# Start-up loads of a two-layer encoder: issued later, and in another order

## The chip, the core and the metric

The kernel runs on one core of one Trainium2 chip. The metric is the device time of one execution in microseconds (us); less is better. The kernel before was timed three times: 567.24, 567.74 and 567.70 us, median 567.7 us. One more execution was profiled; it took 567.6 us, of which the profile's span (first to last instruction) is 565.8 us. All times "at" which something happens below are us from the start of that span.

The engines are named as the profile names them: PE is the matrix engine (PEld its weight loads), DVE the vector engine, ACT the scalar engine, POOL GpSimd, and SP the engine that here does nothing but issue DMAs. "SPq", "POOLq" and "ACTq" are DMAs issued by these engines. In the DMA parts q1 is SP's queue, q10 is ACT's and q0 is POOL's.

## What is computed

A trunk of two residual layers on one sequence of 256 tokens of width 1024, all in float32:

```python
for layer in range(2):
    hn = rms_norm(h, norm_mix_g[layer])
    if layer == 0:
        proj = hn @ ab_w_in                       # q, k, v of mixers A and B
        o_a = gqa_attention(rope(rms(qa)), rope(rms(ka)), va)
        o_b = dilated_attention(qb, kb, vb, rel_bias)
        mix = concat([o_a, o_b]) @ ab_w_out
    else:
        mix = mla_attention(hn, ...) @ c_w_out
    h = h + mix
    hn = rms_norm(h, norm_mlp_g[layer])
    h = h + square(relu(hn @ mlp_w1[layer])) @ mlp_w2[layer]
return rms_norm(h, final_norm_g)
```

The first product of layer 0 needs the input x twice: transposed and multiplied by the norm's gain (that feeds PE), and as token rows (their sums of squares give the norm's factor 1/rms, which is applied behind the product).

## The kernel before

All weights are packed on the host into 1-MiB chunks of 128 partitions x 2048 numbers, in the order of their use: chunks 0 and 1 are the query weights of mixer A ("qA"), chunk 2 its key and value weights ("kvA"), chunks 3 to 6 the query and key weights of mixer B ("qkB"), and so on. The change's title counts them from one: its third and fourth chunk are chunks 2 and 3 here.

A chunk goes through three steps. SP loads it into one of three buffers (tile `raw`, RAW_BUFS = 3). ACT casts a piece of 512 or 1024 columns to the matrix engine's format (`whi`, line 224, `cast_piece`). DVE subtracts that from the raw piece (`wlo`, line 231, `low_piece`). PE then forms each product from three matmuls, hi x hi, hi x lo and lo x hi (`mm3`, lines 277 to 279). When the last piece of chunk i has been split, `low_piece` issues the load of chunk i + 3 into the buffer that has come free (lines 232 and 233).

Each engine works through its instructions in the order in which the program writes them, and so does each DMA issuer. In layer 0 that order is written by hand (`tc.manual_schedule()`): first a loop over kk = 0 to 7 (lines 983 to 1001), one step per 128 rows of x; in each step ACT casts one piece of chunk 0 or 1 and one row block of x, DVE makes the low parts of both, and PE does 6 matmuls of 512 columns. Then kvA with chunk 2, in four quarters `kv(0)` to `kv(3)`, with chunk 3's pieces cast in between, and then a long string of letters (`ORDER_AB`), each a small step.

What is loaded in the first 20 us, beside the chunks:

- `xgt`, x transposed with the gains, in five parts (ACT's queue and SP's);
- `kc`, 0.5 MiB of constants: rotary tables, and the identity matrix for PE's transposes. POOL multiplies its tables with the gains `gaq` (`tables`, lines 782 to 789) into `tab` (tile `early`), which DVE's rotary step `rope_a` (lines 751 to 761) reads;
- `xh`, the token rows of x, 1 MiB. ACT squares them (`squares`, line 345, four instructions: two behind the second piece of chunk 3, two behind the third);
- POOL's three: `gaq` (64 KB), `oh` (66 KB) and `rb` (1 KB), lines 739 to 741. The last two feed one small matmul at line 1022.

Two waits are added by hand. `hold(dma, ins)` (line 298) makes a DMA's issue wait until the instruction `ins` has ended; before the change it is used once, for chunk 2 behind the cast of step kk = 2 (line 991). SP issues in order, so what stands behind a held DMA waits with it.

Of the kernel before, what the change touches and what calls it, by code (L numbers as in the profile page):

```python
# [20 lines left out]
P = 128  # L21
# [13 lines left out]
NUM_BUCKETS = 32  # L35
# [135 lines left out]
def encoder(ctx: ExitStack, tc: tile.TileContext, x, xg, wall, grow, const, onehot, relb, out):  # L171
    nc = tc.nc
    cp = ctx.enter_context(tc.tile_pool(name="cp", bufs=1))
    wp = ctx.enter_context(tc.tile_pool(name="wp", bufs=1))
    ap = ctx.enter_context(tc.tile_pool(name="ap", bufs=1))
# [10 lines left out]
    def s_bank():  # L186
        return psum("s", 2)
# [4 lines left out]
    def o_bank():  # L192
        return psum("o", 2)
# [9 lines left out]


    raws, parts, done = {}, {}, set()
    at = {"take": 0, "piece": 0, "quarter": 0, "low": [], "hand": True}

    def load(i, pieces=1):
        if i >= N_CH:
            return  # L210
        raws[i] = wp.tile([P, CW], F32, name="raw", tag="raw", bufs=RAW_BUFS)
        for q in range(pieces):
            s = slice(q * CW // pieces, (q + 1) * CW // pieces)
            nc.sync.dma_start(raws[i][:, s], wall[i, :, s])

    def cast_piece(cast=nc.scalar.copy):

# [8 lines left out]
    def low_piece():  # L226

        i, q, n = at["low"].pop(0)
        hi, lo = parts[i, q // 2]
        s = slice(512 * (q % 2), 512 * (q % 2 + n))  # L230
        nc.vector.tensor_tensor(lo[:, s], raws[i][:, 512 * q:512 * (q + n)], hi[:, s].bitcast(F32), op=OP.subtract)  # L231
        if q + n == 4:
            load(i + RAW_BUFS)

    def split_piece(cast=nc.scalar.copy):
        cast = cast_piece(cast)
        low_piece()
        return cast
# [16 lines left out]
    def take(name, j, n, whole=True):  # L255

        i = at["take"]
        assert ORDER[i] == (name, j), (ORDER[i], name, j)
        at["take"] += 1
        while whole and at["piece"] < 4 * i + 4:  # L260
            split_piece()

        def operand(k, c=slice(None)):
            half, kk = divmod(k, n // 2)
            return tuple(z.rearrange("p (k c) -> p k c", k=n // 2)[:, kk, c] for z in parts[i, half])

        return i, operand
# [6 lines left out]
    def mm3(out, a, b, first, last):  # L274

        (ah, al), (bh, bl) = a, b
        nc.tensor.matmul(out, ah, bh, start=first, stop=False)  # L277
        nc.tensor.matmul(out, ah, bl, start=False, stop=False)  # L278
        return nc.tensor.matmul(out, al, bh, start=False, stop=last)  # L279
# [4 lines left out]
    def tok(z, k, t):  # L284
        return pair(z, ALL, k, cols(t))
# [5 lines left out]
    def xT(k):  # L291
        return xgt[:, N_G + k * S:N_G + k * S + S]
# [5 lines left out]
    def hold(dma, ins):  # L298

        tc.add_manual_dep(dma.ins, ins.ins.name, mybir.DependencyInfo(  # L300
            mybir.DependencyClass.Sync, mybir.DependencyReason.DATA), reason="hold")
# [9 lines left out]
    kc = cp.tile([P, N_K], F32, name="kc")  # L311
    xh = cp.tile([P, NT, D], F32, name="xh")
# [231 lines left out]
    later = Later()  # L544
# [169 lines left out]
    with tc.tile_pool(name="l0", bufs=1) as lp:  # L714
# [10 lines left out]
        gaq = early[:, 4 * P:]  # L725
# [4 lines left out]
        rb = lp.tile([NUM_BUCKETS + 1, HB], F32, name="rb")  # L730
        OT = [ap.tile([P, KT, S], F32R, name=f"OT{i}", tag=f"OT{i}") for i in range(2)]

        oh = sp.tile([P, 512], F32, name="oh", tag="prob", bufs=3)
        nc.vector.memset(rb, 1.0)
        for s in range(2):
            other = slice(64 - 64 * s, 128 - 64 * s)
            nc.gpsimd.memset(klA[other, s].bitcast(F32), 0.0)
            nc.gpsimd.memset(klB[other, s::2].bitcast(F32), 0.0)
        nc.gpsimd.dma_start(gaq, bass.AP(tensor=grow.tensor, offset=grow.offset, ap=[[0, P], [1, P]]))
        nc.gpsimd.dma_start(oh[:NUM_BUCKETS + 1, :], onehot)  # L740
        nc.gpsimd.dma_start(rb[:NUM_BUCKETS, :], relb)

        bias = {}

# [37 lines left out]
        def tables():  # L782
            for gi in range(2):
                for t in range(NT):
                    cs, sn = kc[:, K_COSA + 64 * t:K_COSA + 64 * t + 64], kc[:, K_SINA + 64 * t:K_SINA + 64 * t + 64]
                    gv = gaq[:, cols(gi, 64)]
                    nc.gpsimd.tensor_tensor(tab[:, 2 * gi, t], cs, gv, op=OP.mult)
                    nc.gpsimd.tensor_tensor(tab[:, 2 * gi + 1, t, 0:32], sn[:, 0:32], gv[:, 32:64], op=OP.mult)
                    nc.gpsimd.tensor_tensor(tab[:, 2 * gi + 1, t, 32:64], sn[:, 32:64], gv[:, 0:32], op=OP.mult)

        def sums_q(t):
            sq = work()
            nc.scalar.activation(sq, acc[t], AF.Square)
            nc.vector.reduce_sum(sums[:, t, 2:10], sq.rearrange("p (h e) -> p h e", e=64), axis=AX.X)
# [34 lines left out]
        def rope_q(t):  # L829
            qr[t] = sp.tile([P, 512], F32, name="qr", tag="prob", bufs=3)  # L830
            rope_a(qr[t], acc[t], HA, 0, t)
# [146 lines left out]
        with tc.manual_schedule():  # L978
            spin = s_bank()
            for _ in range(N_SPIN):  # L980
                nc.tensor.matmul(spin, idle[:, :P], idle, start=True, stop=True)
            nc.gpsimd.tensor_copy(g, xgt[:, :N_G])
            for j in range(2):
                i, w = take("qA", j, 4, whole=False)
                for k in range(4):
                    kk = 4 * j + k
                    gc = xgt[:, G_MIX + kk:G_MIX + kk + 1]
                    cast = split_piece(nc.scalar.copy if kk else nc.vector.tensor_copy)
                    if kk == 2:
                        raws[2] = wp.tile([P, CW], F32, name="raw", tag="raw", bufs=RAW_BUFS)  # L990
                        hold(nc.sync.dma_start(raws[2], wall[2]), cast)
                        nc.sync.dma_start(kc, const)
                    if kk == 4:
                        nc.sync.dma_start(xh, x.rearrange("(t p) d -> p t d", p=P))
                    nc.scalar.activation(hT[0][:, kk], xT(kk), AF.Copy, scale=gc)  # L995
                    nc.vector.scalar_tensor_tensor(hT[1][:, kk], xT(kk), gc, hT[0][:, kk].bitcast(F32),
                                                   op0=OP.mult, op1=OP.subtract)
                    for t in range(NT):
                        mm3(acc[t], tok(hT, kk, t), w(k), kk == 0, kk == 7)
                    at["quarter"] += 1  # L1000
                done.add(i)
            tables()
            i, w = take("kvA", 0, 8, whole=False)

            def kv(q):
                for k in (2 * q, 2 * q + 1):
                    for t in range(NT):
                        mm3(acckv[t][:, :S], tok(hT, k, t), w(k), k == 0, k == 7)
                if q == 3:
                    done.add(i)  # L1010
                at["quarter"] += 1

            def split(n):
                for _ in range(n):
                    split_piece()

            split(4)
            for t in range(NT):
                sums_q(t)
            kv(0)  # L1020
            lines = o_bank()
            nc.tensor.matmul(lines[:HB, :], rb, oh[:NUM_BUCKETS + 1, :], start=True, stop=True)
            split(1)
            rope_q(0)
            kv(1)
            line_d = dp.tile([HB, 2 * S], F32, name="line_d")
            ls = sp.tile([P, 512], F32, name="ls", tag="pts", bufs=3)
            nc.scalar.copy(ls[:HB, :], lines[:HB, :])
            nc.gpsimd.dma_start(line_d, ls[:HB, :])
            split(1)  # L1030
            squares(part, 0, 0)
            squares(part, 0, 1)
            kv(2)
            split(1)
            squares(part, 1, 0)
            squares(part, 1, 1)
            kv(3)
            rope_q(1)
            sums_k()
            norms()  # L1040
            oacc = {}
            steps = {"a": b0, "b": qk_b(1), "v": v_b(), "o": out_first("outA", OT, oacc),
                     **attention_steps([head_a(h) for h in range(HA)] + [head_b(h) for h in range(HB)], OT)}
            once = {"c": cast_piece, "l": low_piece, "d": spread_d, "s": spread, "n": norms_end, "m": scales,
                    "q": lambda: turn_q(0), "r": lambda: turn_q(1), "k": turn_k, "u": values_a, "x": scale_k,
                    "p": lambda: [rope_a(kr[:, t], acckv[t][:, :P], 2, 2, t) for t in range(NT)],
                    "i": lambda: [load_bias(j) for j in range(2)]}
            for c in "".join(ORDER_AB).replace(" ", ""):
                next(steps[c]) if c in steps else once[c]()
            assert all(next(z, "end") == "end" for z in steps.values()) and not at["low"]  # L1050
# [6 lines left out]
    with tc.tile_pool(name="l1", bufs=1) as lp:  # L1057
# [31 lines left out]
        for j in range(2):  # L1089
            i, w = take("down", j, 4)  # L1090
            for n, m in enumerate(order):
                for k in range(4):
                    kk = 4 * j + k
# [157 lines left out]
```

## Time and profile before

| what | value |
|---|---|
| three timed runs, median | 567.7 us (567.24 to 567.74) |
| profiled execution, its own time | 567.6 us |
| its span | 565.8 us |
| PE busy | 556.0 us (98%) |
| PE weight loads busy | 462.0 us (82%) |
| DVE busy | 398.8 us (70%) |
| ACT busy | 329.9 us (58%) |
| POOL busy | 34.2 us (6%) |
| moved by DMA | 97.16 MB, mean 172 GB/s |

PE has work in nearly all of the span, so nearly every microsecond by which PE starts or resumes later is a microsecond at the end. The DMA queues are busy less than half of the time over the span, but not evenly: in the page's 40 slices (14 us each) the first two show a busy share of eight tenths. That is the stretch in which the change acts.

### The profile page before, as it was taken

How to read it: one execution, taken by the hardware profiler on the slowest of the kernel's cores; microseconds unless marked ns; L12 is line 12 of the kernel's file. 1: busy time of each engine (PE TensorE's matmuls, PEld its weight loads, DVE VectorE, ACT ScalarE, POOL GpSimd, SP SyncE). 2: the span in 40 equal slices, each digit the busy share in tenths (PEclk: the TensorE clock that was granted, in tenths of full speed). 3: DMA queues.
4: the chain of work that ended last, by engine and by line, in shares of the span. 5: the costliest groups of instructions: out<-in, count | busy, mean ns of one | idle time of the engine just before them, and what ended most of it. 6: DMA issues, size and time to landing. Idle time of an engine off the chain costs nothing.

```text
span 565.8 us, 8120 instructions
## 1 busy us (share of the span) xinstructions
PE 556.0 (98%) x3044; PEld 462.0 (82%) x3044; DVE 398.8 (70%) x717; ACT 329.9 (58%) x616; POOL 34.2 (6%) x60
## 2 busy tenths in 40 slices
PE   8999999999999999999999999999999999999995
PEld 4899777888888888888889976678888888888884
DVE  4999978986675666566687987578666566756645
ACT  5879878755454454545465797665545545454514
POOL 3430000000000000000012000000000000000003
PEclk9999999999999999999999999999999999999998
DMA  8847344655455455545426222255555455554201
GB/s 281 362 157 240 125 150 156 255 210 199 169 203 200 173 195 181 218 152 218 162 105 246 86 76 75 75 186 167 205 164 208 155 217 191 181 217 155 75 2 74
DMA packets 16663, 97.16 MB, mean 172 GB/s; under 512 B 1858, under 2 KB 3906, under 8 KB 5872
## 3 DMA queue, kind: packets, MB, share of 16 engines
q1 hardware_dynamic: 15040, 94.51, 46.2%
q0 software_dynamic: 864, 1.20, 1.0%
q10 hardware_dynamic: 720, 0.94, 0.5%
q8 instruction: 24, 0.39, 0.3%
q14 instruction: 15, 0.12, 0.1%
HBM read 95.05 MB, written 1.06 MB: 170 GB/s over the span
## 4 chain that ended last, share of the span: by engine, by line
PE 90%; DMA 3%; ACT 3%; DVE 2%; issue 1%; POOL 1%; SPq 0%; POOLq 0%; DVEq 0%; ACTq 0%
PE s L602 20%; PE mm L277 15%; PE mm L279 15%; PE mm L278 15%; PE s L603 10%; PE s L1208 2%; DMA xh<-in_x 2%; PE o L409 2%; PE o L481 1%; PE o L470 1%; DMA raw<-in_wall 1%; PE o L420 1%; PE o L522 1%; PE mm L602 1%; ACT whi L224 1%; PE s L942 1%
## 5 line engine op out<-in xcount | busy, mean ns | idle before, releaser
L231 DVE TENSOR_TENSOR wlo<-raw,whi 128x1024 fp32r<-128x1024 f32 (+1 forms) x182 | 208.9, 1164 | 96.2 <-ACT whi L224 95.6
L224 ACT CAST whi<-raw 128x1024 fp32r<-128x1024 f32 (+1 forms) x181 | 178.1, 1006 | 84.1 <-PE mm L279 39.7
L602 PE MATMUL s<-hTs,whi 128*128 128x512 f32 x480 | 168.6, 393 | 0.1
L603 PE MATMUL s<-hTs,wlo 128*128 128x256 f32 x480 | 134.4, 280 | 0.0
L602 PEld LDWEIGHTS s<-hTs,whi 128*128 128x128 f32 x480 | 90.0, 188 | 20.5 <-DVE hTs L530 0.4
L277 PE MATMUL mm<-whi,h2h 128*128 128x512 f32 x252 | 99.5, 395 | 0.0
L278 PE MATMUL mm<-wlo,h2h 128*128 128x512 f32 x252 | 99.3, 394 | 0.0
L279 PE MATMUL mm<-whi,h2l 128*128 128x512 f32 x252 | 99.0, 396 | 0.0
L603 PEld LDWEIGHTS s<-hTs,wlo 128*128 128x128 f32 x480 | 90.4, 188 | 1.4
L595 ACT CAST h2h<-work 128x256 fp32r<-128x256 f32 x64 | 25.6, 402 | 54.9 <-DVE work L594 54.9
L277 PEld LDWEIGHTS mm<-whi,h2h 128*128 128x128 f32 x252 | 47.5, 188 | 11.5 <-ACT h2h L595 0.9
L279 PEld LDWEIGHTS mm<-whi,h2l 128*128 128x128 f32 x252 | 47.4, 188 | 11.2 <-DVE h2l L596 0.3
L278 PEld LDWEIGHTS mm<-wlo,h2h 128*128 128x128 f32 x252 | 47.5, 188 | 9.4
L592 ACT COPY work<-s 128x256 f32<-128x256 f32 x60 | 22.0, 367 | 46.5 <-PE s L603 46.5
L593 DVE TENSOR_TENSOR work<-s,work 128x256 f32<-128x256 f32 x60 | 25.3, 421 | 17.7 <-ACT work L592 17.7
L596 DVE TENSOR_TENSOR h2l<-work,h2h 128x256 fp32r<-128x256 f32 x64 | 26.8, 422 | 14.2 <-ACT h2h L595 14.2
L594 DVE SCALAR_TENSOR_TENSOR work<-work 128x256 f32<-128x256 f32 x64 | 27.0, 425 | 2.1
L277 PE MATMUL mm<-whi,hTs 128*128 128x256 f32 (+1 forms) x80 | 27.4, 343 | 0.3 <-ACT hTs L995 0.2
L279 PE MATMUL mm<-whi,hTs 128*128 128x256 f32 (+1 forms) x80 | 26.5, 331 | 0.0
L277 PE MATMUL mm<-whi,OT 128*128 128x512 f32 x64 | 26.5, 414 | 0.0
L278 PE MATMUL mm<-wlo,hTs 128*128 128x256 f32 (+1 forms) x80 | 26.4, 330 | 0.0
L278 PE MATMUL mm<-wlo,OT 128*128 128x512 f32 x64 | 25.6, 401 | 0.0
(238 smaller groups left out, 761.9 us busy)
## 6 DMA issues: line engine op xcount, KB each, us to landing
raw<-in_wall SPq DMA_DIRECT2D x84, 1024.0 KB, 4.8
bias<-line_d SPq DMA_DIRECT2D x4, 384.0 KB, 6.0
raw<-in_wall SPq DMA_DIRECT2D x4, 256.0 KB, 5.6
raw<-in_wall SPq DMA_DIRECT2D x2, 512.0 KB, 7.2
xh<-in_x SPq DMA_DIRECT2D x1, 1024.0 KB, 11.1
out<-y SPq DMA_DIRECT2D x2, 320.0 KB, 2.2
xgt<-in_xg SPq DMA_DIRECT2D x2, 256.0 KB, 7.7
kc<-in_const SPq DMA_DIRECT2D x1, 512.0 KB, 8.6
```

The source lines that it names most:

```text
L224: return cast(parts[i, q // 2][0][:, 512 * (q % 2):512 * (q % 2 + n)], raws[i][:, 512 * q:512 * (q + n)])
L231: nc.vector.tensor_tensor(lo[:, s], raws[i][:, 512 * q:512 * (q + n)], hi[:, s].bitcast(F32), op=OP.subtract)
L277: nc.tensor.matmul(out, ah, bh, start=first, stop=False)
L278: nc.tensor.matmul(out, ah, bl, start=False, stop=False)
L279: return nc.tensor.matmul(out, al, bh, start=False, stop=last)
L592: nc.scalar.copy(v[:, 0], bank[:, S:])
L593: nc.vector.tensor_tensor(v[:, 0], bank[:, :S], v[:, 0], op=OP.add)
L594: nc.vector.scalar_tensor_tensor(v[:, 1], v[:, 0], 0.0, v[:, 0], op0=OP.max, op1=OP.mult)
L595: nc.scalar.copy(hi, v[:, 1])
L596: nc.vector.tensor_tensor(lo, v[:, 1], hi.bitcast(F32), op=OP.subtract)
L602: nc.tensor.matmul(bank, wh, hTs[:, k].rearrange("p a t -> p (a t)"), start=k == 0, stop=False)
L603: nc.tensor.matmul(bank[:, S:], wl, hT[0][:, k], start=False, stop=k == 7)
```

## The change

The loads that stand behind chunk 1 are issued at other points of the kk loop.

```diff
-    at = {"take": 0, "piece": 0, "quarter": 0, "low": [], "hand": True}
+    at = {"take": 0, "piece": 0, "quarter": 0, "low": [], "hand": True, "later": True}
...
-            nc.sync.dma_start(raws[i][:, s], wall[i, :, s])
+            dma = nc.sync.dma_start(raws[i][:, s], wall[i, :, s])
+        return dma
...
-        if q + n == 4:
+        if q + n == 4 and not at["later"]:
             load(i + RAW_BUFS)
...
-        nc.gpsimd.dma_start(gaq, bass.AP(tensor=grow.tensor, offset=grow.offset, ap=[[0, P], [1, P]]))
-        nc.gpsimd.dma_start(oh[:NUM_BUCKETS + 1, :], onehot)
-        nc.gpsimd.dma_start(rb[:NUM_BUCKETS, :], relb)
...
                     if kk == 2:
                         raws[2] = wp.tile([P, CW], F32, name="raw", tag="raw", bufs=RAW_BUFS)
                         hold(nc.sync.dma_start(raws[2], wall[2]), cast)
-                        nc.sync.dma_start(kc, const)
-                    if kk == 4:
-                        nc.sync.dma_start(xh, x.rearrange("(t p) d -> p t d", p=P))
+                        hold(nc.gpsimd.dma_start(gaq, bass.AP(tensor=grow.tensor, offset=grow.offset,
+                                                              ap=[[0, P], [1, P]])), cast)
+                        nc.gpsimd.dma_start(oh[:NUM_BUCKETS + 1, :], onehot)
+                        nc.gpsimd.dma_start(rb[:NUM_BUCKETS, :], relb)
+                    if kk == 3:
+                        hold(nc.sync.dma_start(kc, const), cast)
+                    if kk == 6:
+                        hold(load(3), cast)
+                        at["later"] = False
+                    if kk == 7:
+                        hold(nc.sync.dma_start(xh, x.rearrange("(t p) d -> p t d", p=P)), cast)
```

Chunk 3 is no longer issued by `low_piece` of chunk 0's last piece (kk = 3), but at kk = 6. Chunk 4 is still issued by `low_piece`, inside `split_piece` of kk = 7, which is called ahead of the `if kk == 7` that issues the token rows.

No instruction is added or taken away, and PE, ACT and DVE keep their instructions in the same order. Two lists change. First SP's list of DMA issues, from chunk 2 on, before; `raw` is a weight chunk (chunks 2, 3, 4, 5 in the order in which they stand), `kc` the constants, `xh` the token rows:

```order
L991 DMA raw<-in_wall 128x2048 [waits DMAHW3_49,Activation_49]
L992 DMA kc<-in_const 128x1024 [waits DMAHW4_49]
L214 DMA raw<-in_wall 128x2048 [waits DMAHW6_49,DMAHW5_49,DVE_49]
L994 DMA xh<-in_x 128x2x1024
L214 DMA raw<-in_wall 128x2048 [waits DMAHW2_49,DMAHW7_49,DMAHW0_49,DVE_49]
L214 DMA raw<-in_wall 128x2048 [waits DMAHW3_49,DVE_49]
```

The same place of SP's list with the change:

```order
L989 DMA raw<-in_wall 128x2048 [waits DMAHW3_49,Activation_49]
L995 DMA kc<-in_const 128x1024 [waits DMAHW4_49,Activation_49]
L214 DMA raw<-in_wall 128x2048 [waits DMAHW5_49,DMAHW6_49,DVE_49,Activation_49]
L214 DMA raw<-in_wall 128x2048 [waits DMAHW2_49,DMAHW0_49,DVE_49]
L1000 DMA xh<-in_x 128x2x1024 [waits DMAHW7_49]
L214 DMA raw<-in_wall 128x2048 [waits DMAHW3_49,DVE_49]
```

`kc` and chunk 3 now wait for a cast on ACT as well, and chunk 4 and the token rows have changed places. The token rows' own hold shows no ACT wait of its own, since SP has waited for DVE's work on the same piece one row earlier.

Second, POOL's list at its three DMAs, before (`klB` is a buffer that POOL clears, `g` a copy of gains, `early` holds `gaq` and the tables):

```order
L738 MEMSET klB 64x4x256
L739 DMA early<-in_grow 128x128
L740 DMA oh<-in_onehot 33x512
L741 DMA rb<-in_relb 32x8 [waits DVE_49]
L982 COPY g<-xgt 128x36 [waits DMAHW0_49,Pool_49]
```

The same place with the change:

```order
L739 MEMSET klB 64x4x256
L980 COPY g<-xgt 128x36 [waits DMAHW0_49,Pool_49]
L990 DMA early<-in_grow 128x128 [waits Activation_49]
L992 DMA oh<-in_onehot 33x512
L993 DMA rb<-in_relb 32x8 [waits DVE_49]
```

The copy of the gains has come in front, and the three DMAs wait for ACT's cast of step kk = 2. Behind them on POOL stand the tables, as before.

## Rows read from the trace of the kernel before

**Rows 1.** The chain that ended last, first 52 us; start us, us, what

```profile
11.56 11.12 DMA xh<-in_x
...
22.71 0.73 ACT junk L345 x2
...
37.45 0.33 PE o L849
```

**Rows 2.** Timeline of SP from 8 to 17 us; start us, us, instruction, count

```profile
8.71 0.33 SPq L991 DMA_DIRECT2D raw<-in_wall  x1
9.08 0.52 SPq L992 DMA_DIRECT2D kc<-in_const  x1
11.19 0.33 SPq L214 DMA_DIRECT2D raw<-in_wall  x1
11.56 0.43 SPq L994 DMA_DIRECT2D xh<-in_x  x1
16.31 0.33 SPq L214 DMA_DIRECT2D raw<-in_wall  x1
```

**Rows 3.** DMAs issued from 8.7 to 9.5 us; count, KB, us to landing

```profile
raw<-in_wall SPq DMA_DIRECT2D x1, 1024.0 KB, 7.7
kc<-in_const SPq DMA_DIRECT2D x1, 512.0 KB, 8.6
```

**Rows 4.** The same, issued from 11.5 to 12 us

```profile
raw<-in_wall SPq DMA_DIRECT2D x1, 1024.0 KB, 9.0
xh<-in_x SPq DMA_DIRECT2D x1, 1024.0 KB, 11.1
```

**Rows 5.** The same, issued from 16 to 17 us

```profile
raw<-in_wall SPq DMA_DIRECT2D x1, 1024.0 KB, 10.0
```

**Rows 6.** DMA queues from 12 to 22 us: packets, MB, share of 16 engines

```profile
q1 hardware_dynamic: 813, 4.19, 102.6%
```

**Rows 7.** DMA queues from 7 to 10 us

```profile
q1 hardware_dynamic: 271, 0.65, 57.9%
q0 software_dynamic: 108, 0.13, 44.0%
```

**Rows 8.** Timeline of PE; start us, us, line, operation, shape, count

```profile
1.21 5.04 PE L981 MATMUL s<-work 128*128 128x512 bf16 x12 [1.21 <-DVE rb L734]
5.90 0.59 PE L277 MATMUL mm<-whi,hTs 128*128 128x512 f32 x1
...
16.17 0.40 PE L277 MATMUL mm<-whi,hTs 128*128 128x512 f32 x1
...
18.97 0.28 PE L277 MATMUL mm<-whi,hTs 128*128 128x256 f32 x1
...
27.75 0.60 PE L836 MATMUL o<-kc,qr 128*128 128x128 f32 x4
```

**Rows 9.** Timeline of ACT; in brackets idle time before, and its end

```profile
20.17 0.62 ACT L224 CAST whi<-raw 128x512 fp32r<-128x512 f32 x1 [0.40 <-DMA raw<-in_wall]
...
22.71 0.63 ACT L345 ACTIVATE junk<-xh 128x512 bf16<-128x512 f32 x1
...
24.09 0.60 ACT L224 CAST whi<-raw 128x512 fp32r<-128x512 f32 x1
...
28.01 2.18 ACT L224 CAST whi<-raw 128x512 fp32r<-128x512 f32 x4
```

**Rows 10.** Timeline of DVE, from 24 to 27 us

```profile
24.73 0.69 DVE L231 TENSOR_TENSOR wlo<-raw,whi 128x512 fp32r<-128x512 f32 x1 [0.55 <-ACT whi L224]
...
26.72 0.69 DVE L761 TENSOR_TENSOR qr<-qr,work 128x512 f32<-128x512 f32 x1
```

**Rows 11.** Timeline of POOL, from 3 to 18 us

```profile
17.77 0.76 POOL L787 TENSOR_TENSOR early<-kc,early 128x64 f32<-128x64 f32 x1 [11.86 <-DMA kc<-in_const]
```

**Rows 12.** Stretches: us, busy us of each engine, granted clock, DMA share, GB/s

```profile
22.70:34.40 11.70, 11.70 (x101) 11.70 (x101) 10.71 (x21) 11.53 (x23) 7.11 (x8) 1.00 0.58 225
37.00:565.00 528.00, 520.62 (x2842) 434.67 (x2842) 370.87 (x655) 303.69 (x565) 16.92 (x26) 1.00 0.46 164
```

## The prediction

> **What bounds the kernel now.** I read the page first: PE is busy nearly all the time, so only what keeps PE from its work counts. The change touches the first 20 us, so I then read the chain of waits for the first 52 us. The reader should see [rows 1] there: the chain does not run along PE at first. It runs from the transfer of the token rows (xh, issued at 11.56, landed 11.12 later, at 22.7) to ACT's squares at 22.71, 0.03 behind the landing, and from there over ACT and DVE to a PE transpose at 37.45; from then on it is PE. So two things limit the start: PE's own start on chunks 0 and 1, and this chain, whose first link is a landing.
>
> Then the issues and landings. SP issues chunk 2, kc, chunk 3, xh, chunk 4 at 8.71, 9.08, 11.19, 11.56, 16.31 [rows 2]. They land 7.7, 8.6, 9.0, 11.1 and 10.0 later [rows 3 to 5], that is at 16.4, 17.7, 20.2, 22.7 and 26.3. The landings stand in the order of issue, 1.3 us apart for kc's half MiB and 2.5 us for each MiB of chunk 3 and xh, whatever the issues' own distances were. From 12 to 22 the queue q1 alone keeps all 16 DMA engines busy (102.6%) and moves 4.19 MB in 10 us [rows 6]. So q1 is a line: what is issued later neither takes bandwidth from what stands ahead nor lands before it, and a load's landing is set by its place in the line.
>
> Last PE's own start [rows 8]. The 48 matmuls of the kk loop go from 5.90 to 18.97, 13.07 us. Where nothing stops them, 12 of them take 18.97 - 16.17 = 2.80, or 0.233 each; 48 would take 11.2. So PE loses 1.9 us there, waiting for pieces of chunks 0 and 1.
>
> **The change part by part.** *POOL's three held behind the cast of kk = 2.* From 7 to 10 us q0 takes 44.0% of 16 engines, 1.3 us of all of them, for 0.13 MB, while q1 comes down to 57.9% [rows 7]. That is when the last pieces of chunk 0 are due. Without it these pieces and chunk 1 land some 1.3 us earlier, and PE ends the kk loop earlier: by 1.9 us at most (all its loss) and by 0 at least (if the start of the transfers limits it). I take 1.2, since the burst's own 1.3 us is the nearest row, and chunk 1's second half now meets the burst. None of it reaches the end, for a reason that follows below.
>
> *The burst itself* moves from 7 to 10 us to some 3 to 4 us later and takes its 1.3 us there, from chunk 1's end or chunk 2. What waits for POOL's three is not late: the tables start at 17.77, when kc is there [rows 11], and kc keeps its place behind chunk 2. So kc's and POOL's holds cost nothing as long as the line ahead of them is not empty; chunk 2's and chunk 3's holds likewise, since at 13 to 14 us, when kk = 6's cast ends, chunk 2 and kc are still to come. If a hold did empty the line, each microsecond of that would be one for all that follows. SP queues nothing else behind these holds than the loads themselves.
>
> *Chunk 4 before the token rows.* This is the part that counts. Up to xh the line before holds chunks 0 to 3, the transposed x, kc and xh. With the change chunk 4 goes ahead, 1 MiB more. A lower bound for xh's new landing is 22.7 + 2.5 = 25.2 (one MiB at the line's pace). An upper one is 26.3: the two have changed places, so xh comes where chunk 4 came, with the same bytes ahead and behind the same burst. The burst may be cheaper in its new place, by 1.3 at most; then 23.9. I take 26.0, nearest to the row of chunk 4, because that is a landing in this very place. It is 3.3 us later than 22.7.
>
> What chunk 4 gains is worth nothing: it is first cast at 28.01, after 26.3, and ACT does not wait for it [rows 9].
>
> Who is behind xh? ACT works in order. Behind the squares stand the cast of chunk 3's third piece (24.09), the rest of the squares, the first casts of the queries, all of chunk 4 [rows 9]. DVE's low part of that piece waits for the cast (24.73, 0.55 idle), and behind it stands the second rotary step, which ends with the row at 26.72 [rows 10]. PE turns its result at 27.75 [rows 8]. From 22.70 to 34.40 ACT is busy 11.53 of 11.70 us and DVE 10.71 [rows 12], so neither has room to make up 3.3 us before the transpose at 37.45.
>
> So ACT will stand from about 21.5 until 26.0. PE, 1.2 us early, runs out of work at 27.75 - 1.2 = 26.5 and stands until 27.75 + 3.3 = 31: there the early gain is lost, whatever it was. Everything behind starts 3.3 late. After 37 PE is busy 520.6 of 528 us [rows 12], its loads are gated by its own progress, and nothing there gives time back.
>
> **Sum.** 567.6 (the profiled execution; the median of the timed runs is 567.7) + 3.3 = 570.9 us. By the bounds of the landing: 25.2 gives 570.1, 26.5 (a little over the row) gives 571.4.
>
> **The rivals.**
>
> *The clock falls in the hole.* PE is to stand for over 4 us at about 26 to 31. The trace of before has no such hole behind 5.9, and shows the granted clock at 1.00 in all stretches there [rows 12]. At the start, behind idle time, 12 matmuls of 512 columns took 5.04 us, 0.42 each, against 0.233 later [rows 8]. If PE comes back that slow for as long, it loses 12 x 0.187 = 2.2 us more: 573.1 us. For it: the length of the hole. Against it: the slow stretch need not be as long, and PE is not needed at full speed while ACT and DVE catch up. The Trainium skill, page "TensorE: Matmul & The Clock Gate", section "HAM oscillation — how this bites in real kernels", says that waits for a DMA can send PE back to its lower clock, and that the work behind the wait then starts slow; no stretch of this trace shows it.
>
> *The burst is cheap in its new place.* Part of its cost may have come from meeting ACT's queue and small packets. If the line is ahead by 1.3, xh lands at 24.7 to 23.9, and the end moves by 1.2 to 2.0: 569.2 us in the middle.
>
> *Time is given back later.* Some wait behind 37 us that is not bound to PE's progress takes up most of the 3.3 us: about 568 us, no change. Against it: nothing in [rows 12] leaves more than 7.4 us of PE idle over 528 us, and that in pieces.
>
> *The other side: loads share the bandwidth.* If outstanding loads of one queue ran side by side, holding back kc, chunk 3 and xh would speed up chunks 1 and 2, and xh would not have to wait for chunk 4. Then ACT would reach the squares with xh there as soon as its own work lets it, 1.2 us earlier than 22.71 with PE's early start, and all follows: 567.6 - 1.2 = 566.4 us, faster. It decides from the point at which xh lands before 22.7. Against it: the landings in order and 2.5 us apart [rows 3 to 5].
>
> **How the numbers follow.** Differences under 0.2% (1.1 us) can't be told from no change by a measurement of this kernel. Forecast, chunk 4 ahead of xh: 0.67, 570.9 us. Clock: 0.11, 573.1. Cheap burst: 0.10, 569.2. Given back: 0.07, 568. Sharing: 0.05, 566.4. The first three are slower by over 0.2%: 0.88. I take 0.02 off for what I have not thought of, so slower 0.86, same 0.08, faster 0.06. The range of the forecast alone is 570.1 to 571.4. For 8 in 10 I reach down to the cheap burst and up to a clock loss of some 1.5 us: 569.0 to 572.6.
>
> **What would show it.** In the profile after: xh issued behind chunk 4 and landed at 25.2 to 26.5; ACT's first square idle before it for 4 to 5 us, ended by DMA xh; a hole of PE of about 4 us that ends with the transpose of line 836 by DVE's second rotary step; the transpose that was at 37.45 some 3 us later; q0 gone from 7 to 10 us, and PE at kvA's first matmul (18.97 before) about 1.2 us earlier. The granted clock behind the hole decides the first rival. The forecast is wrong if xh lands before 24, if ACT does not wait for it, or if PE's distance to before shrinks again behind 40 us.

## The result, and the profile after

The changed kernel takes 571.29 us (median of 4 runs, 571.11 to 572.80), the kernel before 567.48 (4 runs). The ratio is 1.0069 [1.0058, 1.0081]: slower by 0.7%, 3.8 us. The execution that the profiler recorded is the one at 572.80, with a span of 571.0; the other three have spans of 569.3 to 569.5. So the trace of after explains 5.2 us of span (571.0 - 565.8), of which some 3.6 are typical. Where the recorded one lost the 1.5 us by which it is longer can't be read, since no other was recorded.

**The chain of waits** answers to [rows 1]. First 60 us of after; start us, us, what:

```profile
15.56 11.35 DMA xh<-in_x
26.94 0.73 ACT junk L346 x2
...
30.94 0.70 DVE qr L759
31.69 1.12 PE o L834 x4
```

The same transfer still leads it, but it is issued at 15.56 and lands at 26.9, where it landed at 22.7. The transposes of the queries' second half (L834, L836 before) run at 31.69 (27.75 before).

**The issues** of SP answer to [rows 2]; timeline of after, 8 to 17 us:

```profile
8.43 0.33 SPq L989 DMA_DIRECT2D raw<-in_wall  x1
9.52 0.33 SPq L995 DMA_DIRECT2D kc<-in_const  x1
13.40 2.11 SPq L214 DMA_DIRECT2D raw<-in_wall  x2
15.56 0.43 SPq L1000 DMA_DIRECT2D xh<-in_x  x1
```

The two of L214 are chunks 3 and 4. **The landings** of the last two issues (15.1 to 15.7 us; count, KB, us to landing) answer to [rows 4, 5]:

```profile
raw<-in_wall SPq DMA_DIRECT2D x1, 1024.0 KB, 7.6
xh<-in_x SPq DMA_DIRECT2D x1, 1024.0 KB, 11.3
```

Chunk 4 lands at 15.19 + 7.6 = 22.8, where xh used to land, and xh 4.1 us behind it.

**ACT** answers to [rows 9]; timeline of after, in brackets the idle time before and what ended it:

```profile
26.94 0.63 ACT L346 ACTIVATE junk<-xh 128x512 bf16<-128x512 f32 x1 [4.98 <-DMA xh<-in_x]
...
40.54 1.07 ACT L841 ACTIVATE kr<-kr,fa 128x64 f32<-128x64 f32 x4 [1.80 <-DVE fa L816]
42.99 0.76 ACT L850 CAST kdA<-o 64x256 fp32r<-64x256 f32 x2 [1.39 <-PE o L847]
```

The first square waits 4.98 us for xh. **DVE** answers to [rows 10]:

```profile
28.95 0.69 DVE L232 TENSOR_TENSOR wlo<-raw,whi 128x512 fp32r<-128x512 f32 x1 [4.59 <-ACT whi L225]
...
30.94 0.69 DVE L759 TENSOR_TENSOR qr<-qr,work 128x512 f32<-128x512 f32 x1
```

DVE waits 4.59 us for the cast that stands behind the squares on ACT, and the second rotary step ends at 31.6. **PE** answers to [rows 8]:

```profile
17.85 0.28 PE L278 MATMUL mm<-whi,hTs 128*128 128x256 f32 x1
...
26.61 0.28 PE L280 MATMUL mm<-whi,hTs 128*128 128x256 f32 x1
31.69 1.12 PE L834 MATMUL o<-kc,qr 128*128 128x128 f32 x4 [4.80 <-DVE qr L759]
...
32.82 0.41 PE L279 MATMUL mm<-wlo,hTs 128*128 128x256 f32 x1
33.03 0.41 PE L280 MATMUL mm<-whi,hTs 128*128 128x256 f32 x1
```

PE reaches kvA's first matmul at 17.85 (18.97 before), 1.1 us early, and then stands for 4.80 us. Behind the hole the matmuls of 256 columns begin 0.21 us apart and take 0.41 each; ahead of the hole they begin 0.12 apart and take 0.28. That is the clock, and **the stretches** show it (us, busy us of PE, PEld, DVE, ACT and POOL, granted clock, DMA share, GB/s):

```profile
27.00:29.00 2.00, 0.00 (x0) 0.00 (x0) 0.05 (x1) 1.97 (x6) 0.00 (x0) 1.00 0.07 29
29.10:31.60 2.50, 0.00 (x0) 0.00 (x0) 2.47 (x6) 2.47 (x8) 1.04 (x3) 0.50 0.00 0
31.60:35.80 4.20, 4.11 (x19) 4.11 (x20) 3.90 (x9) 4.10 (x9) 3.72 (x5) 0.50 0.47 156
36.00:40.00 4.00, 4.00 (x36) 4.00 (x35) 3.87 (x13) 2.67 (x3) 1.85 (x1) 1.00 0.30 102
```

While PE stands, the granted clock goes from 1.00 to 0.50, the 1.2 GHz level, and it stays there for the first 4.2 us of PE's work; then it is 1.00 again.

**The queues**, 7 to 10 us and then 12 to 16 us of after, answer to [rows 7] (packets, MB, share of 16 engines):

```profile
q1 hardware_dynamic: 485, 1.19, 100.6%
...
q1 hardware_dynamic: 181, 1.08, 68.3%
q0 software_dynamic: 101, 0.13, 27.3%
```

POOL's three are gone from 7 to 10 us, and q1 moves 1.19 MB there instead of 0.65. They run from 12 to 16 us and take 27.3% of 4 us, 1.1 us of all engines (1.3 before).

So the 5.2 us of span are: squares at 26.94 instead of 22.71, +4.2; and about 1.0 more behind the slow clock. The latter is seen at ACT's kdA casts (L850, L852 before), which wait for PE's transposes of the keys. The same rows of before:

```profile
36.33 1.06 ACT L843 ACTIVATE kr<-kr,fa 128x64 f32<-128x64 f32 x4 [1.93 <-DVE fa L818]
37.82 0.76 ACT L852 CAST kdA<-o 64x256 fp32r<-64x256 f32 x2 [0.42 <-PE o L849]
```

The kr steps come 4.2 us later than before (40.54 against 36.33), the casts 5.2 later (42.99 against 37.82). From kr step to cast it is 1.49 us in before and 2.45 in after.

### The profile page after: what moved, and what is told of

The parts are those of the page before. It is cut to its first block, busy times and chain, and to the rows that moved or that the text cites. A ratio compares the mean times of both kernels' runs of the same rounds, so it can differ in the third digit from the quotient of the medians.

```text
span 571.0 us, 8120 instructions
## 1 busy us (share of the span) xinstructions
PE 557.0 (98%) x3044; PEld 463.7 (81%) x3044; DVE 398.8 (70%) x717; ACT 329.7 (58%) x616; POOL 33.8 (6%) x60
## 4 chain that ended last, share of the span: by engine, by line
PE 91%; DMA 4%; ACT 2%; DVE 2%; POOL 1%; issue 0%; SPq 0%; POOLq 0%; DVEq 0%; ACTq 0%
PE s L603 19%; PE mm L278 16%; PE mm L280 16%; PE mm L279 16%; PE s L604 10%; PE s L1214 2%; DMA xh<-in_x 2%; PE o L410 2%; PE o L482 1%; PE o L471 1%; PE o L421 1%; DMA raw<-in_wall 1%; PE o L523 1%; PE mm L603 1%; DMA xgt<-in_xg 1%; PE s L940 1%
## 5 line engine op out<-in xcount | busy, mean ns | idle before, releaser
L278 PEld LDWEIGHTS mm<-whi,h2h 128*128 128x128 f32 x252 | 47.5, 188 | 11.5 <-ACT h2h L596 0.9
L278 PE MATMUL mm<-whi,hTs 128*128 128x256 f32 (+1 forms) x80 | 27.9, 349 | 0.0
L280 PE MATMUL mm<-whi,hTs 128*128 128x256 f32 (+1 forms) x80 | 27.2, 340 | 0.0
```

## The experiments

The theory (A in the expectations) is the prediction's: the place of xh in the line is all of it, and the holds and POOL's three matter only as far as they change that place. Against it stands that the holds, or POOL's three in their new place, bring part of the loss. Two questions stand beside them: what the slow clock costs, and whether PE's earlier start can be used. The timed runs stand beside runs of the kernel before (567.69 us, 23 runs, for the first four; 567.54, 27 runs, for the last four).

**1. Token rows ahead of chunk 4** (all else as after).

```diff
                     if kk == 6:
                         hold(load(3), cast)
-                        at["later"] = False
                     if kk == 7:
                         hold(nc.sync.dma_start(xh, ...), cast)
+                        at["later"] = False
+                        load(4)
```

> The change as it is, with one order turned back: the token rows (xh) are issued ahead of chunk 4, all holds kept. Theory A, place in the line: xh lands 2.5 to 4 us earlier than with the change (26.9), at 23 to 24.5, PE's hole goes to under 1 us, the clock stays at 1.00, and the time comes back to 567 to 568.5 us. Rival B, the holds: xh is late because it is issued 4 us later than before (15.6 against 11.6) and the holds let the line run dry; then xh still lands at 26 or later and the time stays at about 571.

Measured: 567.77 us, ratio 1.0002 [0.9993, 1.0010]. Issue and landing of xh, the first square, the stretch behind it:

```profile
14.29 0.38 SPq L999 DMA_DIRECT2D xh<-in_x  x1
```

```profile
xh<-in_x SPq DMA_DIRECT2D x1, 1024.0 KB, 8.2
```

```profile
22.51 0.63 ACT L346 ACTIVATE junk<-xh 128x512 bf16<-128x512 f32 x1 [0.92 <-DMA xh<-in_x]
```

```profile
31.00:36.50 5.50, 5.50 (x47) 5.31 (x45) 5.00 (x18) 3.59 (x6) 2.44 (x1) 1.00 0.49 174
```

The whole loss is gone, and the clock stays at 1.00. xh is issued 2.7 us later than before (14.29 against 11.56) and lands at the same time (22.5 against 22.7), a little earlier than I had expected. So with POOL's three late, as here, all holds together cost nothing and gain nothing, and the rival falls.

**2. The swap alone** in the kernel before.

```diff
-                    if kk == 4:
+                    if kk == 7:
                         nc.sync.dma_start(xh, ...)
```

> The kernel before with one edit: xh is issued at kk = 7, behind chunk 4, without any hold; POOL's three, kc and chunk 3 stay where they were. Theory A: the swap alone makes the loss: xh lands at 25.2 to 27, the time is 570.5 to 571.8 us, as with the whole change. Rival B: without the holds the line stays full, xh lands within 1 us of 22.7 and the time is 567 to 568.5 us.

Measured: 571.90 us, ratio 1.0068 [1.0055, 1.0081], as much as the whole change (and 0.1 us above the time that I had expected). Landings of chunk 4 and xh (issued at 16.3 and 16.70), the first square, PE's hole, the stretch behind:

```profile
raw<-in_wall SPq DMA_DIRECT2D x1, 1024.0 KB, 6.3
xh<-in_x SPq DMA_DIRECT2D x1, 1024.0 KB, 9.6
```

```profile
26.32 0.63 ACT L345 ACTIVATE junk<-xh 128x512 bf16<-128x512 f32 x1 [3.66 <-DMA xh<-in_x]
```

```profile
31.07 0.66 PE L836 MATMUL o<-kc,qr 128*128 128x128 f32 x4 [3.16 <-DVE qr L761]
```

```profile
28.00:31.00 3.00, 0.00 (x0) 0.00 (x0) 2.63 (x6) 2.96 (x9) 1.05 (x3) 1.00 0.00 0
31.00:33.50 2.50, 2.43 (x17) 2.43 (x18) 2.42 (x7) 2.47 (x5) 2.02 (x4) 0.78 0.24 26
33.50:36.50 3.00, 3.00 (x18) 3.00 (x18) 2.74 (x5) 2.94 (x5) 3.00 (x2) 0.62 0.81 330
```

xh takes the landing that chunk 4 had in before (26.3, [rows 5]), which was the upper bound of the prediction. Squares are 3.6 us later, the span (570.0) 4.2. The other 0.6 is the clock's, which falls here only when PE is at work again: from kr step to kdA cast it is 2.08 us (39.93 and 42.01), 0.59 more than before.

**3. POOL's three early again** (all else as after).

```diff
+        nc.gpsimd.dma_start(gaq, ...)
+        nc.gpsimd.dma_start(oh[:NUM_BUCKETS + 1, :], onehot)
+        nc.gpsimd.dma_start(rb[:NUM_BUCKETS, :], relb)
...
-                        hold(nc.gpsimd.dma_start(gaq, ...), cast)
-                        nc.gpsimd.dma_start(oh[:NUM_BUCKETS + 1, :], onehot)
-                        nc.gpsimd.dma_start(rb[:NUM_BUCKETS, :], relb)
```

> The change with POOL's three back at their old place at the start. Theory A: what POOL's three gave PE (its matmuls of chunks 0 and 1 done some 1.5 us earlier) is lost in the hole anyway, so the time is that of the change within 0.5 us, 570.8 to 571.8; the hole of PE is shorter by the 1 to 2 us that PE comes later, and the clock may then stay at 1.00. Rival: holding POOL's three is itself part of the loss (tables late); then this is faster than the change by 1 us or more.

Measured: 570.82 us, ratio 1.0061 [1.0048, 1.0074], no different from after. Its profiled execution (573.06) is its longest, as that of after was; there xh lands at 27.7, and:

```profile
32.49 0.78 PE L837 MATMUL o<-kc,qr 128*128 128x128 f32 x3 [3.90 <-DVE qr L762]
```

```profile
32.50:36.00 3.50, 3.50 (x17) 3.50 (x18) 3.42 (x7) 3.44 (x7) 3.01 (x4) 0.52 0.42 112
```

PE ended the kk loop at 19.65 here, 1.8 us later than in after, and its hole is 0.9 shorter, though xh lands 0.8 later: what POOL's three give or take at the start is taken or given back in the hole. That the clock might stay up behind the shorter hole was a miss. The late xh shows what the prediction said of a hold that lets the line run dry. ACT's cast of kk = 6 is late as well, so chunk 3 is issued at 15.22 instead of 13.40; from 16 to 17 us q1 moves 0.23 MB, in after 0.43. That the holds do this is read from one execution; the timed runs show no loss by it.

**4. POOL's three late, in the kernel before.** The other half of the change by itself.

```diff
-        nc.gpsimd.dma_start(gaq, ...)      (and oh, rb)
...
                         hold(nc.sync.dma_start(raws[2], wall[2]), cast)
+                        hold(nc.gpsimd.dma_start(gaq, ...), cast)      (and oh, rb)
                         nc.sync.dma_start(kc, const)
```

> The kernel before with POOL's three held behind the cast of kk = 2, and nothing else. Theory A: PE ends chunks 0 and 1 some 1.5 us earlier, but xh still lands at 22.5 to 24, and the chain from xh over ACT and DVE sets the end: 567 to 568.5 us, no gain clear of 0.2%. Rival: PE's start bounds the kernel; then 566 to 566.5 us.

Measured: 567.55 us, ratio 1.0001 [0.9993, 1.0010]. The end of the kk loop and the transposes, then the first square:

```profile
17.55 0.28 PE L277 MATMUL mm<-whi,hTs 128*128 128x256 f32 x1
...
27.30 0.66 PE L833 MATMUL o<-kc,qr 128*128 128x128 f32 x4 [0.60 <-DVE qr L758]
```

```profile
22.54 0.63 ACT L345 ACTIVATE junk<-xh 128x512 bf16<-128x512 f32 x1 [0.92 <-DMA xh<-in_x]
```

PE is 1.4 us early at the loop's end, and xh comes only 0.2 earlier: the burst still runs ahead of it. At the transposes PE waits 0.60 us for DVE and is only 0.45 ahead of before (27.30 against 27.75); the time shows nothing of it.

**5. The hole filled.** After, with 40 matmuls of 256 columns on constants ahead of the late transposes; their result is used nowhere.

```diff
+            def keep_on():
+                fill, o16 = s_bank(), ones.bitcast(BF16)
+                for _ in range(40):
+                    nc.tensor.matmul(fill[:, :256], o16[:, :P], o16, start=True, stop=True)
...
-"r": lambda: turn_q(1)
+"r": lambda: (keep_on(), turn_q(1))
```

> The change, with 40 matmuls of 256 columns on constants (their result is not used) put into PE's hole, ahead of the transposes of the second rotary step. They take some 4.3 us, the hole was 4.8. Theory A, loss = late token rows + a part for the clock: the granted clock stays at 1.00 behind the hole, xh still lands at 26 to 27, and the time comes down from about 571.3 by 0.3 to 1.2 us, to 570.1 to 571.0. Rival: the slow clock costs nothing since PE waits anyway; then 571.0 to 571.6, as with the change.

Measured: 570.88 us, ratio 1.0060 [1.0047, 1.0073]. The filling, the square, the stretches:

```profile
27.90 4.54 PE L1050 MATMUL s<-ones 128*128 128x256 bf16 x40
```

```profile
26.68 0.63 ACT L346 ACTIVATE junk<-xh 128x512 bf16<-128x512 f32 x1 [3.43 <-DMA xh<-in_x]
```

```profile
27.60:31.00 3.40, 3.40 (x33) 3.05 (x33) 2.27 (x5) 3.37 (x11) 0.69 (x3) 1.00 0.04 14
31.00:36.50 5.50, 5.50 (x50) 5.38 (x48) 5.16 (x10) 5.40 (x10) 5.02 (x5) 1.00 0.54 188
```

With PE kept at work the clock stays at 1.00, and the span (569.6) is 3.8 us longer than before, squares 4.0 later: nothing comes on top. From kr step to kdA cast it is 1.49 us again (40.30 and 41.79), as in before, so the 1.0 of after is the clock's, although the filling holds the transposes up to 32.28. In the medians the filling brings 0.4 us (571.29 to 570.88), and the two intervals overlap, so by the timed runs the clock's share is not clear of zero.

**6. Fewer bytes ahead of xh.** If only the place counts, half of kc (columns 256 to 767, used in layer 1 alone) can go behind chunk 4. Built on experiment 4.

```diff
-                        nc.sync.dma_start(kc, const)
+                        nc.sync.dma_start(kc4[:, 0::3], const4[:, 0::3])
...
+                    if kk == 7:
+                        nc.sync.dma_start(kc4[:, 1:3], const4[:, 1:3])
```

> Toward a faster version: the kernel before with POOL's three held (as e4), and the half of kc that layer 0 does not need (256 KB) issued behind chunk 4. Theory A, the line in front of xh sets the chain: chunk 3 and xh land 0.6 us earlier than in e4 (20.0 and 22.5), and the end moves by -0.3 to -0.7 us against e4: 566.8 to 567.3. Rival: with xh earlier, ACT's own work sets the chain at once; then no change.

Measured: 566.91 us, ratio 0.9992 [0.9983, 1.0001]. The first square:

```profile
21.50 0.63 ACT L345 ACTIVATE junk<-xh 128x512 bf16<-128x512 f32 x1 [0.53 <-DMA xh<-in_x]
```

xh lands 1.0 us earlier than in experiment 4. Not all of that is the edit's: chunk 2, which stands ahead of the moved half of kc, lands 0.5 earlier already (15.9 against 16.4). That leaves some 0.6 for a quarter MiB less, as I had expected. The time just fails to show a gain.

**7. Work ahead of the squares.** Experiment 4 with the first two squares moved behind the cast of chunk 3's third piece.

```diff
-            squares(part, 0, 0)
-            squares(part, 0, 1)
             kv(2)
             split(1)
+            squares(part, 0, 0)
+            squares(part, 0, 1)
```

> e4 with the first two squares of the token rows moved behind ACT's cast of chunk 3's third piece, so that ACT does that cast while it would wait for xh. Theory A: PE's hole of 0.6 us ahead of the second rotary step's transposes goes, and ACT's wait for xh shrinks by 0.5: -0.3 to -0.6 us against e4, 566.9 to 567.3. Rival: ACT and DVE are full from 22.7 to 34.4 and the order within makes no difference: 567.5.

Measured: 567.10 us, ratio 1.0000 [0.9991, 1.0009]: no change that can be told. The median lies in the range of theory A, but the runs spread from 566.54 to 568.91, and their mean (567.50) is that of the kernel before (567.52). The square still waits, with less time lost, and PE no longer waits ahead of the transposes (0.60 in experiment 4):

```profile
22.60 0.63 ACT L345 ACTIVATE junk<-xh 128x512 bf16<-128x512 f32 x1 [0.40 <-DMA xh<-in_x]
```

```profile
26.81 0.66 PE L833 MATMUL o<-kc,qr 128*128 128x128 f32 x4
```

So the hole went as theory A said; in the time the interval covers both the theory and the rival.

**8. Both, 6 and 7.**

> e6 and e7 together: xh 0.6 us earlier and not waited for by the cast. Theory A: the sum of both, -0.7 to -1.2 us against e4, 566.3 to 566.9, faster than before by 0.15 to 0.25%. Rival: another link of the chain (POOL's norm factors, which need all squares) takes over and it stays at 567 or more.

Measured: 566.64 us, ratio 0.9990 [0.9981, 0.9999]. The landing, the square, the transposes:

```profile
xh<-in_x SPq DMA_DIRECT2D x1, 1024.0 KB, 11.6
```

```profile
21.84 0.63 ACT L345 ACTIVATE junk<-xh 128x512 bf16<-128x512 f32 x1
```

```profile
26.69 0.66 PE L833 MATMUL o<-kc,qr 128*128 128x128 f32 x4 [0.18 <-DVE qr L758]
```

ACT no longer waits for xh ahead of the first square, and PE waits 0.18 us for its transposes. It has the lowest median here, 0.1% under the kernel before by the ratio, which is under the 0.2% that the prediction took for the least that can be told; the interval's upper end is 0.9999, and it overlaps with that of experiment 6.

## Why the prediction was right, and where its sizes were off

*The line.* Right. Chunk 4 and xh changed places (22.8 and 26.9 for 26.3 and 22.7), experiment 2 does it alone, and experiment 1 undoes it alone. The rival that loads share the bandwidth falls with them: xh landed at the same time whether issued at 11.56 or at 14.29, and in after chunk 4 and xh, issued 0.4 us apart, landed 4.1 apart. The landings go by the place in the line, whichever load stands there (us; experiments 1 and 2):

| place | before | after | 1 | 2 |
|---|---|---|---|---|
| chunk 3 | 20.1 | 20.3 | 20.0 | 20.1 |
| the next | xh 22.7 | chunk 4 22.8 | xh 22.5 | chunk 4 22.6 |
| the one behind | chunk 4 26.3 | xh 26.9 | chunk 4 25.8 | xh 26.3 |
| chunk 5 | 28.6 | 29.4 | 28.3 | 28.6 |

The Trainium skill, page "DMA: Bandwidth & Descriptors", section "🔬 Queues, rings and completion order", has the descriptors of one ring consumed in their order on each DMA engine, and warns that a later one may finish its write first; the loads of this table landed in the order of their issue.

*The size of +3.3.* Too small: the squares came 4.2 us later. The term that was mis-sized is xh's landing, 26.0 taken for 26.9 here (26.3 in experiment 2, 26.7 in experiment 5). I had taken a value a little under the upper bound, though the row of chunk 4 in that very place said 26.3, and chunk 4 had landed 3.6 behind the load ahead of it, not 2.5. Where the rest comes from the trace shows. Its semaphore updates count a load's landing in 16 steps, as many as there are DMA engines. In after 15 steps of xh are counted by 25.30, 2.5 us behind chunk 4, as the line's pace has it; the last comes at 26.91. From 25.0 to 26.4 one engine still moves packets of 4 KB, the rows of xh, while the others move the 8-KB packets of chunk 5, which stands behind xh. So xh waits for one engine that is behind the others. The last step of chunk 4 in before comes late too (25.18, then 26.27), and so does that of xh in experiment 2 (25.17, then 26.30): the row for this place held one late step, and in after it is 0.5 us worse.

Why one engine is late is not shown. In that stretch one engine has a packet of instructions to move (after, 23.0 to 25.3 us):

```profile
q1 hardware_dynamic: 185, 0.95, 102.8%
q8 instruction: 1, 0.02, 2.9%
```

2.9% of 16 engines over 2.3 us is 1.1 us of one engine. Such a packet stands between 22 and 26 us in every run, but the trace does not name a packet's engine, and in experiment 4 the last step of chunk 4 comes only 0.2 us behind the others. It remains a guess that no experiment tried.

*ACT stands, DVE and PE follow.* Right in each step: 4.98 us idle, ended by xh; 4.59 on DVE; 4.80 on PE, ended by DVE's second rotary step (4 to 4.5 forecast).

*POOL's three.* Right: 1.1 us early at the end of the kk loop (1.2 taken), and nothing of it left behind the hole. Experiments 3 and 4 show both directions. The burst cost 1.1 us in its new place, so the rival of a cheap burst falls.

*The clock.* The rival that was given 0.11 came about, beside the forecast and not in its place. Its price was wrong: 2.2 us forecast, 0.6 to 1.0 in the profiled executions of after and experiment 2, nothing left when the hole is filled (2.45 and 2.08 us from kr step to kdA cast, against 1.49 before and with the hole filled), and 0.4 in the medians, not clear of zero. What the prediction held against it fits the rows: from 31.60 to 35.80 ACT is busy 4.10 of 4.20 us and DVE 3.90, so PE is not alone on the path while it is slow; the 2.2 us had taken every slow matmul as lost time. The Trainium skill, page "TensorE: Matmul & The Clock Gate", section "HAM oscillation — how this bites in real kernels", says that the work behind a wait for a DMA may start at the lower clock; the trace of after now agrees, with 0.50 granted, while in experiment 2 PE's first 1.3 us behind the hole still ran at 1.00.

*Given back later.* It did not happen: 4.2 us at the squares, 5.2 at the end.

*The total.* 570.9 forecast, 571.29 measured. Two misses lie in it, of one sign: 0.9 at the landing and up to 1.0 of the clock. In the profiled execution they add to all of its 572.8; in the other three runs their sum must be smaller, about 0.3 (spans of some 569.4 - 565.8 = 3.6, less 3.3), and which of the two shrank there was not recorded. So the line and who waits for it are shown; that the sum came within 0.4 us of the median, with both terms too small in the recorded execution, is in part luck.

## What to carry to other kernels

Read the loads of one queue as a line: sort them by when somebody waits for them, and count the bytes ahead of the load that the chain of waits begins with, since here the time of its issue changed nothing and its place 3.6 to 4.2 us: 2.5 for the MiB ahead, the rest because the last of the 16 steps of its landing came late. "In the order of use" has to mean the order in which an engine would stand without them: chunk 4 had 1.7 us to spare in before, xh none, and putting the one with room ahead of the one without cost the kernel 0.7%. A gain at the start (PE 1.1 to 1.4 us early) is worth nothing until the next wait moves as well; experiment 4 shows it waiting, and experiments 6 and 8, where xh lands earlier too, move the time by 0.1% at most.

## What the runs showed of the hardware

- Behind a single hole of PE (3.16 us in experiment 2, 3.90 in 3, 4.80 in after), in a kernel that otherwise keeps it 98% busy, the granted clock was 0.50, the 1.2 GHz level, instead of 1.00. In after it fell while PE stood, in experiment 2 only after PE had begun again (1.00 from 28 to 31 us, 0.78 and 0.62 behind it). With 40 matmuls for nothing in the hole it stayed at 1.00.
- The lower clock cost 1.0 us in after and 0.6 in experiment 2, read from kr step to kdA cast; in after it covered the first 4.2 us of PE's work behind the hole.
- POOL's three small loads (0.13 MB) took 1.1 to 1.3 us of all 16 engines in either place; q1 moved 0.65 MB beside them in 3 us and 1.19 MB without them.
- A load of 1 MiB landed 2.5 us behind the one ahead of it, but 3.6 to 4.1 us where the last of its 16 steps of landing came 1.1 to 1.6 us behind the other 15 (chunk 4 in before, xh in after and in experiment 2). Chunk 5 stood behind it in the line each time.
